# The scans of a stick-breaking attention cut at pairs of key tiles, done in place, and queued across steps

## The chip, the cores and the metric

One core of one Trainium2 chip runs the whole program. Its engines run side by side, each through its own list of instructions in order: TensorE (PE, with its weight loads as PEld), VectorE (DVE), ScalarE (ACT), GpSimd (POOL), and SyncE (SP), which issues most transfers. The metric is the time of one execution in device microseconds (us), the median over several runs.

## The reference

A decoder layer over 1024 tokens of width 1024, in float32: a gated feed-forward half, two attentions side by side, a second feed-forward half, and a gated embedding. The change touches one of the two attentions, the stick-breaking one, with 8 heads of width 64:

```python
def one_block(args):                  # 128 queries against all keys
    qi, pi = args
    z = jnp.einsum('bqhd,bkhd->bhqk', qi, k).astype(jnp.float32) * scale
    mask = kpos[None, :] < pi[:, None]
    log_beta = jax.nn.log_sigmoid(z)
    log_1m = jnp.where(mask, jax.nn.log_sigmoid(-z), 0.0)
    after = lax.cumsum(log_1m, axis=3, reverse=True) - log_1m
    a = jnp.where(mask, jnp.exp(log_beta + after), 0.0)
    return jnp.einsum('bhqk,bkhd->bqhd', a.astype(v.dtype), v)
```

So the weight of key s for query t is sigmoid(z[t,s]) times the product of sigmoid(-z[t,j]) over all keys j between s and t. The kernel has no logarithm: it scans the sigmoid(-z) of a query from its own position back to key 0, as a running product, and multiplies the result with sigmoid(z).

## The kernel before

Products are made of matmuls in a reduced float32 form, with each operand split into a high and a low part, three matmuls for one. The attention part goes over 16 heads (h = 0 to 15), first the 8 of the forgetting attention, then the 8 stick-breaking ones (h = 8 to 15). A head is four steps, c = 0 to 3; step c handles the two query tiles i = 2c and i = 2c + 1, of 128 queries each, against the first (i + 1) * 128 keys. Work is staggered: step c calls `scores` for its own two tiles and then `apply` for the step before it. So `apply` of c = 3 runs in the next head's step c = 0.

`scores`, for each of its two tiles: PE makes z (lines 941 and 942, two matmuls for each stretch of at most 512 keys); ACT writes sigmoid(-z) to G (L949) and sigmoid(z) to T (L950); POOL zeroes what is above the diagonal in T (L956, AFFINE_SELECT); DVE scans G into R (all scans are recorded at L917); POOL multiplies T with R (L964, L968). The scan begins with the 128 keys of the diagonal, which needs a mask tile as second operand, and goes on backwards from there. The scans and multiplications of a tile are cut in two near the middle (`right` and `left`). For the first tile of a step both parts are issued at once; for the second they are put into the list `later` and issued one after each transposition of `apply`.

`apply`, for the step before: for each pair of key tiles, from the last (kpair = c) down to 0, PE transposes four (for kpair = c three) blocks of T into one of two PSUM banks (L993), ACT copies the high part (L995), DVE subtracts for the low part (L996). A bank is free for the next transposition but one when both have read it. Then PE multiplies the transposed weights with the values (L1015); ACT and DVE bring the result into Y (L1037, L1038).

All PE instructions keep the order in which the program states them. The scans, the low parts (L996) and the splits of the finished Y (L105 on ACT, L106 on DVE) are tied in that order on DVE. Other instructions of ACT, DVE and POOL are placed by a planner with its own estimates of time.

Between these pieces PE does other work, the filling: projections for later heads and gate products (L700, L708) and, in the last head, the output projection (L1227). `take` hands it out in portions: a step has 7, 4, 5 and 6 portions for c = 0 to 3, two of them in `scores`, and `share` says which part of the head's filling the step gets. The filling brings work to the other engines: a new weight tile is copied on ACT for its high part (L129) and subtracted on POOL for its low part (L139); a finished product is evacuated (L782 and L783, L828, L830).

In the last two heads finished rows of Y come back from memory and are split into high and low (`split_y`): two in (h = 14, c = 3), two in (15, 0) and three in (15, 1). The buffers they go into are those of the filling's operand; the second pair becomes free when the last L708 matmul has run.

Of the kernel before, what the change touches and what calls it, by code (L numbers as in the profile page):

```python
# [14 lines left out]
ALU = mybir.AluOpType  # L15
# [3 lines left out]
P = 128  # L19
S = 1024  # L20
# [16 lines left out]
def tile_hybrid_decoder_layer(  # L37
# [6 lines left out]
    nc = tc.nc  # L44
# [871 lines left out]
    def scan(*args):  # L916
        order("dve", nc.vector.tensor_tensor_scan(*args))  # L917

    def scores(step, fill, later=None):
        step["pr"] = []  # L920
        Q, KH, KL = step["st"]["st"]
        fox = step["fox"]
        for i in (2 * step["c"], 2 * step["c"] + 1):
            n = (i + 1) * P
            na, w = seg(n)
            d0 = n - P
            T = slot("T", [P, S])
            if fox:
                m = stat([P, 3], "m")
                l = stat([P, 1], "l")  # L930
                fb = step["fb"]["t"]
                nc.gpsimd.tensor_add(T[:, d0:n], fb[:, d0:n], mask_fox[:])
                nm_ = 0
            else:
                G = slot("GF", [P, S])
                R = slot("RN", [P, S])
            for a in range(na):
                c0, c1 = a * w, (a + 1) * w
                ps = bank("sc")
                q = Q[:, i * P:(i + 1) * P]  # L940
                pe(nc.tensor.matmul(ps[:, :w], q, KH[:, c0:c1], start=True, stop=False))  # L941
                pe(nc.tensor.matmul(ps[:, :w], q, KL[:, c0:c1], start=False, stop=True))  # L942
                if fox:
                    for x0, x1, add in ((c0, min(c1, d0), fb), (max(c0, d0), c1, T)):
                        if x0 < x1:
                            nc.vector.tensor_tensor_reduce(T[:, x0:x1], add[:, x0:x1], ps[:, x0 - c0:x1 - c0], -1.0, m[:, nm_ - 1:nm_] if nm_ else 3e38, ALU.add, ALU.min, m[:, nm_:nm_ + 1])
                            nm_ += 1
                else:
                    nc.scalar.activation(G[:, c0:c1], ps[:, :w], AF.Sigmoid, scale=-(HD ** -0.5))  # L949
                    nc.scalar.activation(T[:, c0:c1], ps[:, :w], AF.Sigmoid, scale=HD ** -0.5)  # L950
            if fox:
                nc.scalar.activation(T[:, :n], T[:, :n], AF.Exp, bias=m[:, nm_ - 1:nm_], scale=-1.0, accum_out=l[:])
                nc.vector.reciprocal(l[:], l[:])  # L953
                nc.gpsimd.tensor_mul(T[:, :n], T[:, :n], l[:].broadcast_to([P, n]))  # L954
            else:
                nc.gpsimd.affine_select(T[:, d0:n], T[:, d0:n], [[-1, P]], ALU.is_ge, 0.0, base=-1, channel_multiplier=1)  # L956
                cut = (i + 1) // 2 * P if i > 2 else 0

                def right(T=T, G=G, R=R, n=n, d0=d0, cut=cut):
                    z0 = max(d0, 1)  # L960
                    scan(R[:, z0 - 1:n - 1][:, ::-1], G[:, z0:n][:, ::-1], mask_sb[:, z0 - d0:P][:, ::-1], 1.0, ALU.mult, ALU.max)
                    if d0:
                        scan(R[:, cut:d0 - 1][:, ::-1], G[:, cut + 1:d0][:, ::-1], G[:, cut + 1:d0][:, ::-1], R[:, d0 - 1:d0], ALU.mult, ALU.bypass)
                    nc.gpsimd.tensor_mul(T[:, cut:n - 1], T[:, cut:n - 1], R[:, cut:n - 1])  # L964

                def left(T=T, G=G, R=R, cut=cut):
                    scan(R[:, 0:cut][:, ::-1], G[:, 1:cut + 1][:, ::-1], G[:, 1:cut + 1][:, ::-1], R[:, cut:cut + 1], ALU.mult, ALU.bypass)
                    nc.gpsimd.tensor_mul(T[:, :cut], T[:, :cut], R[:, :cut])  # L968
                parts = [right, left] if cut else [right]
                if i % 2 and later is not None:  # L970
                    later.extend(parts)
                else:
                    for part in parts:
                        part()
            step["pr"].append(T)
            fill()

    def apply(step, fill, later=()):
        c = step["c"]
        v2 = step["v"]["v"]  # L980
        hd = step["head"] % 4
        av = bank("av")
        pts = {}

        def transposes(kpair):
            width = 512 if kpair < c else 384
            ps = bank("pt")
            for kb in (2 * kpair, 2 * kpair + 1):
                for j in range(2):
                    if kb == 2 * c + 1 and j == 0:  # L990
                        continue
                    col = (kb % 2) * 256 + (j * P if kb < 2 * c + 1 else 0)
                    pe(nc.tensor.transpose(ps[:, col:col + P], step["pr"][j][:, kb * P:(kb + 1) * P], identf[:]))  # L993
            pt = slot("PT", [P, 2, 512], F32R)
            high = nc.scalar.copy(pt[:, 0, :width], ps[:, :width])  # L995
            low = nc.vector.tensor_sub(pt[:, 1, :width], ps[:, :width], f(pt[:, 0, :width]))  # L996
            if not step["fox"]:
                order("dve", low)
                order("act", high)
            pts[kpair] = pt  # L1000

        def values(kpair):
            pt = pts[kpair]
            mm = []
            for kb in (2 * kpair, 2 * kpair + 1):
                for b in range(2):
                    c0 = (kb % 2) * 256
                    if kb < 2 * c + 1:
                        mm.append((av[:, 0:256], v2[:, kb, hd, :], pt[:, b, c0:c0 + 256]))
                    else:  # L1010
                        mm.append((av[:, P:256], v2[:, kb, hd, :], pt[:, b, c0:c0 + P]))
            if kpair == c:
                mm = [mm[0], mm[2], mm[3], mm[1]]
            for i, (o, lh, r) in enumerate(mm):
                pe(nc.tensor.matmul(o, lh, r, start=(kpair == c and i == 0), stop=(kpair == 0 and i == 3)))  # L1015

        def turn_and_scan(kpair):
            transposes(kpair)
            if later:
                later.pop(0)()  # L1020
            fill()

        turn_and_scan(c)
        for kpair in range(c - 1, -1, -1):
            turn_and_scan(kpair)
            if kpair + 2 <= c:
                values(kpair + 2)
# [9 lines left out]
        nc.scalar.copy(ys, av[HD:P, :256])  # L1037
        nc.vector.tensor_add(ys, av[0:HD, :256], ys)  # L1038
        if hh == 1 and c == 3 and step["last"] is False:
            nc.sync.dma_start(yd[Y["idx"]], Y["t"][:])  # L1040
# [38 lines left out]
    def attention():  # L1079
# [80 lines left out]
        for h in range(16):  # L1160
            fox = h < 8
            if h % 2 == 0:
                idx = fox_pairs[h // 2] if fox else 4 + (h - 8) // 2
                ys[h // 2] = {"t": slot("Y", [P, S]), "idx": idx}
            head = ys[h // 2]["idx"] % 4 * 2 + h % 2
            v = (vf1, vf0, vs0, vs1)[h // 4]
            load_fb(h + 1)
            total = sum(u[0] for u in fill[h])
            state = [0.0, 0.0, 0]
            share = (7 / 22, 4 / 22, 5 / 22, 6 / 22) if fox else (0.14, 0.19, 0.29, 0.38)  # L1170
            gens = [u[1] for u in fill[h]]

            def take(last=False):
                state[0] += total * share[state[2]] / (7, 4, 5, 6)[state[2]]
                while gens and (last or state[1] < state[0]):
                    cost = next(gens[0], None)
                    if cost is None:
                        gens.pop(0)
                    else:
                        state[1] += cost  # L1180
            for c in range(4):
                y0, y1 = Y_AT.get((h, c), ((), ()))
                split_y(*y0)
                load_y(*y1)
                step = {"fox": fox, "c": c, "head": head, "st": stacks[h], "v": v, "y": ys[h // 2], "last": h == 15}
# [365 lines left out]
```

## Time and profile before

| | us |
|---|---|
| median of 3 runs | 2271.35 (2271.24 to 2271.48) |
| the profiled execution | 2270.28 |
| its span, first to last instruction | 2268.5 |
| PE busy in the span | 2246.3 |
| DVE busy | 1443.7 |
| ACT busy | 961.6 |
| POOL busy | 827.8 |

The profile shows one execution. Its timeline gives each instruction's start and duration in us, with the idle time before it and what ended that idle time in brackets; its groups gather instructions of one line and form, with their count, busy time, mean duration in ns, and idle time before them; its windows give each engine's busy time in a stretch; its chain follows the work that ended last back from the end. A shape 128x256 stands for 128 partitions of 256 elements. The stick-breaking heads lie between 1052 and 1390 us of the span, about 41 us each.

### The profile page before, as it was taken

How to read it: one execution, taken by the hardware profiler on the slowest of the kernel's cores; microseconds unless marked ns; L12 is line 12 of the kernel's file. 1: busy time of each engine (PE TensorE's matmuls, PEld its weight loads, DVE VectorE, ACT ScalarE, POOL GpSimd, SP SyncE). 2: the span in 40 equal slices, each digit the busy share in tenths (PEclk: the TensorE clock that was granted, in tenths of full speed). 3: DMA queues.
4: the chain of work that ended last, by engine and by line, in shares of the span. 5: the costliest groups of instructions: out<-in, count | busy, mean ns of one | idle time of the engine just before them, and what ended most of it. 6: DMA issues, size and time to landing. Idle time of an engine off the chain costs nothing.

```text
span 2268.5 us, 30573 instructions
## 1 busy us (share of the span) xinstructions
PE 2246.3 (99%) x11462; PEld 1910.0 (84%) x11462; DVE 1443.7 (64%) x2167; ACT 961.6 (42%) x1709; POOL 827.8 (36%) x762
## 2 busy tenths in 40 slices
PE   8999999999999999999999999999999999999999
PEld 6888888888899999988888878888888888888888
DVE  8845555688862355556666675889655555778753
ACT  6333333333353445545555564246333333434431
POOL 2444444300033456554556554410544444200121
PEclk9999999999999999999999999999999999999999
DMA  3232323484334332232224245822423232756132
GB/s 140 101 117 87 123 84 125 151 304 169 105 123 130 111 94 76 74 103 74 76 71 130 70 158 174 303 106 64 139 84 126 84 126 83 263 194 215 61 103 84
DMA packets 192774, 283.87 MB, mean 125 GB/s; under 512 B 28137, under 2 KB 110441, under 8 KB 192626
## 3 DMA queue, kind: packets, MB, share of 16 engines
q1 hardware_dynamic: 192624, 281.92, 37.4%
q8 instruction: 90, 1.47, 0.3%
q14 instruction: 58, 0.48, 0.1%
q10 hardware_dynamic: 2, 0.00, 0.0%
HBM read 189.83 MB, written 75.27 MB: 117 GB/s over the span
## 4 chain that ended last, share of the span: by engine, by line
PE 95%; DVE 3%; ACT 1%; issue 1%; DMA 0%; DVEq 0%; ACTq 0%
PE ps L473 35%; PE ps L368 21%; PE ps L708 11%; PE ps L700 8%; PE ps L1494 4%; PE ps L1227 4%; PE ps L1015 3%; PE ps L993 3%; PE ps L942 1%; PE ps L428 1%; PE ps L941 1%; PE ps L860 1%; PE ps L228 1%; DVE H L106 0%; ACT H L105 0%
## 5 line engine op out<-in xcount | busy, mean ns | idle before, releaser
L368 PE MATMUL ps<-H,H 128*128 128x512 f32 x2184 | 497.7, 389 | 1.2 <-DVE X L376 1.2
L368 PEld LDWEIGHTS ps<-H,H 128*128 128x128 f32 x2184 | 409.3, 188 | 86.7 <-issue 2.0
L473 PE MATMUL ps<-H,WL 128*128 128x512 f32 x1008 | 239.3, 389 | 0.8 <-ACT WL L105 0.8
L473 PEld LDWEIGHTS ps<-H,WL 128*128 128x128 f32 x1008 | 189.1, 188 | 40.5 <-ACT WL L105 1.2
L708 PE MATMUL ps<-H,WH 128*128 128x512 f32 x768 | 211.6, 402 | 0.0
L139 POOL TENSOR_TENSOR WL<-RAW,WH 128x512 fp32r<-128x512 f32 (+1 forms) x108 | 127.6, 1205 | 84.9 <-ACT WH L129 71.2
L708 PEld LDWEIGHTS ps<-H,WH 128*128 128x128 f32 x768 | 136.3, 189 | 22.3 <-issue 0.2
L139 POOL TENSOR_TENSOR WL<-Y,WH 128x512 fp32r<-128x512 f32 (+1 forms) x10 | 14.4, 1464 | 382.6 <-ACT WH L129 382.6
L473 PE MATMUL ps<-H,Q 128*128 128x512 f32 x600 | 143.1, 389 | 0.0
L376 DVE SCALAR_TENSOR_TENSOR X<-ps,X 128x512 f32<-128x512 f32 x168 | 109.0, 685 | 50.9 <-PE ps L368 50.9
L996 DVE TENSOR_TENSOR PT<-ps,PT 128x512 fp32r<-128x512 f32 (+1 forms) x160 | 100.7, 631 | 59.7 <-ACT PT L995 59.4
L473 PEld LDWEIGHTS ps<-H,Q 128*128 128x128 f32 x600 | 112.6, 188 | 23.4
L700 PE MATMUL ps<-WH,H 128*128 128x256 f32 (+1 forms) x896 | 129.8, 286 | 0.0
L995 ACT CAST PT<-ps 128x512 fp32r<-128x512 f32 (+1 forms) x160 | 87.1, 546 | 85.3 <-PE ps L993 79.7
L473 PE MATMUL ps<-X,WL 128*128 128x512 f32 x504 | 121.1, 389 | 0.0
L700 PEld LDWEIGHTS ps<-WH,H 128*128 128x128 f32 x896 | 116.7, 190 | 1.0
L473 PEld LDWEIGHTS ps<-X,WL 128*128 128x128 f32 x504 | 94.6, 188 | 19.6
L708 PE MATMUL ps<-H,WL 128*128 128x512 f32 x384 | 106.1, 396 | 0.0
L917 DVE TENSOR_TENSOR_SCAN RN<-GF,RN 128x127 f32<-128x127 f32 (+2 forms) x96 | 103.3, 1076 | 2.7
L954 POOL TENSOR_TENSOR T<-T,l 128x128 f32<-128x128 f32 (+3 forms) x64 | 73.1, 1150 | 87.2 <-DVE l L953 87.0
L1015 PE MATMUL ps<-PT,X 128*128 128x256 f32 (+1 forms) x640 | 98.2, 282 | 3.8 <-DVE PT L996 2.3
L1015 PEld LDWEIGHTS ps<-PT,X 128*128 128x128 f32 x640 | 90.3, 190 | 13.1 <-DVE PT L996 4.1
(396 smaller groups left out, 4629.7 us busy)
## 6 DMA issues: line engine op xcount, KB each, us to landing
hidden<-PT SPq DMA_DIRECT2D x40, 512.0 KB, 3.1
WH<-in_ffn_w_gate_dram SPq DMA_DIRECT2D x38, 512.0 KB, 5.3
Q<-hidden SPq DMA_DIRECT2D x24, 512.0 KB, 6.9
hidden<-RN SPq DMA_DIRECT2D x22, 512.0 KB, 2.6
RAW<-in_w_in_dram SPq DMA_DIRECT2D x22, 512.0 KB, 4.1
KH<-in_ffn_w_up_dram SPq DMA_DIRECT2D x20, 512.0 KB, 6.2
KL<-in_ffn_w_up_dram SPq DMA_DIRECT2D x20, 512.0 KB, 6.7
T<-in_ffn_w_down_dram SPq DMA_DIRECT2D x20, 512.0 KB, 4.2
```

What stands on the lines that cost most here:

```text
L139: ins = eng_lo.tensor_sub(lo[part], raw[part], f(hi[part]))
L368: pe(nc.tensor.matmul(groups[g][t][:], act[:, a, k, t * P:(t + 1) * P], wt[:, b, k, :], start=(fresh and n == 0), stop=(i in (6, 1, 4) and ...
L376: nc.vector.scalar_tensor_tensor(xs, groups[g][t][:], scale, xs, ALU.mult, ALU.add)
L473: pe(nc.tensor.matmul(ps[:], hl[:, a, k, :], rhs(m, b, k), start=(first and i == 0), stop=(final and i == 11), skip_group_check=True))
L700: pe(nc.tensor.matmul(ps[:, :n], hT[t // 4][a][:, k, (t % 4) * P:(t % 4 + 1) * P], w[k // 4][b][:, k % 4, :n], start=(i == 0), stop=(i == ...
L708: pe(nc.tensor.matmul(ps[:], w[a][:, k, :], hT[half][b][:, k, :], start=(i == 0), stop=(i == 23)))
L917: order("dve", nc.vector.tensor_tensor_scan(*args))
L995: high = nc.scalar.copy(pt[:, 0, :width], ps[:, :width])
L996: low = nc.vector.tensor_sub(pt[:, 1, :width], ps[:, :width], f(pt[:, 0, :width]))
L1015: pe(nc.tensor.matmul(o, lh, r, start=(kpair == c and i == 0), stop=(kpair == 0 and i == 3)))
L1227: pe(nc.tensor.matmul(ps[:], w[a][:, k, :], yT[g][b][:, k, half * 512:half * 512 + 512], start=(i == 0), stop=(i == 11)))
L1494: pe(nc.tensor.matmul(ps, hT[t // 4][a][:, k, (t % 4) * P:(t % 4 + 1) * P], pl["w"][d, k // 2][b][:, k % 2, cs], start=(i == 0), stop=(i = ...
```

## The change

R is gone: the scan writes its product over its own operand in G, and G alternates between the two kinds of buffers that G and R had. A tile's scan and its multiplication are cut at every 256 keys (a pair of key tiles) instead of once near the middle. The part of the diagonal (kp = c) is issued at once for both tiles. The other c parts of a tile go into a queue `pend`, which lives across steps and heads and is kept sorted by step and then from the last pair to the first. `pop()` issues the first of the queue: once after each tile in `scores` and once after each transposition in `apply`; `pop(key)` issues all up to a key, so that a pair's parts are ahead of its transposition. The shares of the filling for the stick-breaking heads become 0.22, 0.20, 0.30 and 0.28 for c = 0 to 3. The description of the change also says "with all gates in the filling"; the diff has no line on gates, and the units of the filling and their order are the same.

```diff
+    def pop(upto=None):
+
+        while pend and (upto is None or pend[0][:2] <= upto):
+            pend.pop(0)[2]()
+            if upto is None:
+                break
+
+    pend = []
+
-    def scores(step, fill, later=None):
+    def scores(step, fill):
...
             else:
-                G = slot("GF", [P, S])
-                R = slot("RN", [P, S])
+                G = slot(("GF", "RN")[i % 2], [P, S])
...
-                cut = (i + 1) // 2 * P if i > 2 else 0
-
-                def right(T=T, G=G, R=R, n=n, d0=d0, cut=cut):
-                    z0 = max(d0, 1)
-                    scan(R[:, z0 - 1:n - 1][:, ::-1], G[:, z0:n][:, ::-1], mask_sb[:, z0 - d0:P][:, ::-1], 1.0, ALU.mult, ALU.max)
-                    if d0:
-                        scan(R[:, cut:d0 - 1][:, ::-1], G[:, cut + 1:d0][:, ::-1], G[:, cut + 1:d0][:, ::-1], R[:, d0 - 1:d0], ALU.mult, ALU.bypass)
-                    nc.gpsimd.tensor_mul(T[:, cut:n - 1], T[:, cut:n - 1], R[:, cut:n - 1])
-
-                def left(T=T, G=G, R=R, cut=cut):
-                    scan(R[:, 0:cut][:, ::-1], G[:, 1:cut + 1][:, ::-1], G[:, 1:cut + 1][:, ::-1], R[:, cut:cut + 1], ALU.mult, ALU.bypass)
-                    nc.gpsimd.tensor_mul(T[:, :cut], T[:, :cut], R[:, :cut])
-                parts = [right, left] if cut else [right]
-                if i % 2 and later is not None:
-                    later.extend(parts)
-                else:
-                    for part in parts:
-                        part()
+
+                def part(kp, T=T, G=G, n=n, d0=d0):
+                    c0 = kp * 256
+                    c1 = min(c0 + 256, n)
+                    z0 = max(c0, 1)
+                    if c1 == n:
+                        z1 = max(d0, 1)
+                        g = G[:, z1:n][:, ::-1]
+                        scan(g, g, mask_sb[:, z1 - d0:P][:, ::-1], 1.0, ALU.mult, ALU.max)
+                        if z0 < d0:
+                            g = G[:, z0:d0][:, ::-1]
+                            scan(g, g, g, G[:, d0:d0 + 1], ALU.mult, ALU.bypass)
+                        c1 = n - 1
+                    else:
+                        g = G[:, z0:c1][:, ::-1]
+                        scan(g, g, g, G[:, c1:c1 + 1], ALU.mult, ALU.bypass)
+                    nc.gpsimd.tensor_mul(T[:, c0:c1], T[:, c0:c1], G[:, c0 + 1:c1 + 1])
+                part(step["c"])
+                pend.extend((step["id"], -kp, lambda kp=kp, part=part: part(kp)) for kp in range(step["c"] - 1, -1, -1))
+                pend.sort(key=lambda e: e[:2])
+                pop()
...
         def turn_and_scan(kpair):
             transposes(kpair)
-            if later:
-                later.pop(0)()
+            pop()
+            pop((step["id"], 2 - kpair))
             fill()

+        pop((step["id"], 1 - c))
         turn_and_scan(c)
...
-        for part in later:
-            part()
...
-            share = (7 / 22, 4 / 22, 5 / 22, 6 / 22) if fox else (0.14, 0.19, 0.29, 0.38)
+            share = (7 / 22, 4 / 22, 5 / 22, 6 / 22) if fox else (0.22, 0.2, 0.3, 0.28)
...
-                later = []
                 state[2] = c
-                scores(step, take, later if prev is not None else None)
+                scores(step, take)
                 if prev is not None:
-                    apply(prev, take, later)
+                    apply(prev, take)
                 prev = step
```

More of the change, by code (lines that the diff above doesn't have):

```diff
@@ L975, in scores, with apply @@
+                part(step["c"])
+                pend.extend((step["id"], -kp, lambda kp=kp, part=part: part(kp)) for kp in range(step["c"] - 1, -1, -1))
+                pend.sort(key=lambda e: e[:2])
+                pop()
             step["pr"].append(T)
             fill()
-    def apply(step, fill, later=()):
+    def apply(step, fill):
         c = step["c"]
@@ L1184, in attention @@
                 load_y(*y1)
[L1185 removed]
+                step = {"fox": fox, "c": c, "head": head, "st": stacks[h], "v": v, "y": ys[h // 2], "last": h == 15, "id": 4 * h + c}
                 if fox:
                     step["fb"] = fbs[h]
[L1188 removed]
                 state[2] = c
[L1190 removed]
+                scores(step, take)
                 if prev is not None:
[L1192 removed]
+                    apply(prev, take)
                 prev = step
```

## The prediction

> **What bounds the kernel now.** I read the page's busy times first, then its chain of work, then windows over the stages.
>
> ```profile
> span 2268.5 us, 30573 instructions
> PE 2246.3 (99%) x11462; PEld 1910.0 (84%) x11462; DVE 1443.7 (64%) x2167; ACT 961.6 (42%) x1709; POOL 827.8 (36%) x762
> PE 95%; DVE 3%; ACT 1%; issue 1%; DMA 0%; DVEq 0%; ACTq 0%
> ```
> ```profile
> 755.00:1055.00 300.00, 295.01 (x2099) 274.19 (x2098) 169.60 (x553) 153.27 (x338) 171.16 (x174) 1.00 0.31 85
> 1055.00:1301.00 246.00, 246.00 (x1431) 215.32 (x1430) 165.14 (x228) 132.98 (x277) 141.80 (x157) 1.00 0.33 88
> 1301.00:1392.00 91.00, 87.13 (x466) 73.37 (x465) 64.87 (x88) 56.53 (x113) 46.54 (x53) 1.00 0.52 169
> ```
>
> The window rows give stretch, length, then busy PE, PEld, DVE, ACT, POOL, the clock and DMA. Heads 8 to 13 (1055 to 1301 us) have PE busy without a gap: 246.00 of 246.00, at full clock. The change removes no matmul, so nothing can be won there. Heads 14 and 15 have 91.00 - 87.13 = 3.87 us of idle PE. PE's timeline shows it as two waits, both in head 15, both for a low part; DVE's shows what held that up.
>
> ```profile
> 1335.84 0.22 PE L941 MATMUL ps<-KH,Q 128*128 128x128 f32 x1
> ...
> 1340.89 0.66 PE L993 MATMUL ps<-identf,T 128*128 128x128 f32 x4 [1.56 <-DVE PT L996]
> ...
> 1345.52 0.34 PE L941 MATMUL ps<-KH,Q 128*128 128x384 f32 x1
> ...
> 1351.38 0.45 PE L1015 MATMUL ps<-PT,X 128*128 128x256 f32 x2
> 1354.13 0.50 PE L1015 MATMUL ps<-PT,X 128*128 128x128 f32 x2 [2.31 <-DVE PT L996]
> ```
> ```profile
> 1336.65 0.42 DVE L1038 TENSOR_TENSOR Y<-ps,Y 64x256 f32<-64x256 f32 x1 [2.09 <-ACT Y L1037]
> 1337.60 2.36 DVE L106 TENSOR_TENSOR H<-X,H 128x1024 fp32r<-128x1024 f32 x2 [0.54 <-ACT H L105]
> 1339.88 0.51 DVE L917 TENSOR_TENSOR_SCAN RN<-GF,mask_sb 128x127 f32<-128x127 f32 x1
> 1340.31 0.53 DVE L996 TENSOR_TENSOR PT<-ps,PT 128x384 fp32r<-128x384 f32 x1
> ...
> 1348.37 3.59 DVE L106 TENSOR_TENSOR H<-X,H 128x1024 fp32r<-128x1024 f32 x3 [1.24 <-PE ps L708]
> ...
> 1353.55 0.53 DVE L996 TENSOR_TENSOR PT<-ps,PT 128x384 fp32r<-128x384 f32 x1
> ```
>
> The most that can be gained is 3.87 us, 0.17%; all else is a question of new waits.
>
> **The change part by part.** Prices, from the groups of DVE and POOL in the scans' stretch:
>
> ```profile
> L917 DVE TENSOR_TENSOR_SCAN RN<-GF,mask_sb 128x128 f32<-128x128 f32 x56 | 36.6, 653 | 14.7 <-ACT GF L949 14.6
> ...
> L917 DVE TENSOR_TENSOR_SCAN RN<-GF,RN 128x255 f32<-128x255 f32 x24 | 23.9, 996 | 0.8
> ...
> L996 DVE TENSOR_TENSOR PT<-ps,PT 128x384 fp32r<-128x384 f32 x33 | 18.2, 552 | 14.4 <-ACT PT L995 14.2
> ...
> L917 DVE TENSOR_TENSOR_SCAN RN<-GF,RN 128x256 f32<-128x256 f32 x16 | 12.6, 787 | 0.6
> ...
> L917 DVE TENSOR_TENSOR_SCAN RN<-GF,RN 128x127 f32<-128x127 f32 x16 | 8.0, 502 | 0.6
> ```
> ```profile
> L139 POOL TENSOR_TENSOR WL<-RAW,WH 128x512 fp32r<-128x512 f32 x32 | 43.1, 1367 | 5.6 <-issue 5.3
> ...
> L968 POOL TENSOR_TENSOR T<-T,RN 128x256 f32<-128x256 f32 x16 | 12.1, 754 | 0.0
> L968 POOL TENSOR_TENSOR T<-T,RN 128x512 f32<-128x512 f32 x8 | 10.4, 1295 | 9.3 <-DVE RN L917 9.3
> ```
>
> *More and smaller pieces.* Scans go from 160 to 192 and multiplications from 104 to 160, over the same elements. A scan's fixed part is 502 - 127 * (787 - 502)/129 = 221 ns, so 32 more are 7.1 us of DVE; a multiplication's is 2 * 754 - 1295 = 213 ns, so 56 more are 11.9 us of POOL. Spread over 337 us, with DVE 67% and POOL 58% busy in the second window, both are hidden: 0. Without that cover they would cost the whole 19 us. Scanning in place has no row; I take the rows of G to R (a tenth more or less on 787 ns would be 0.08 us a piece, 24 pieces a head, 1.9 us, beside a DVE idle for a third of the window). Dropping R frees buffers nobody waits for. ACT's and SP's instructions are the same in number; SP only exchanges neighbours.
>
> *The filling.* In the order of PE's instructions, the filling matmuls between the start of a step c = 3 and its third transposition go from 8 + 7 + 8 + 7 = 30 to 5 + 6 + 6 + 5 = 22; in c = 0 from 10 to 16 (head 15: 9 to 14). So c = 3 gets tighter and c = 0 looser.
>
> *The order on DVE.* This decides. In c = 3 the low part after the first transposition came behind the first tile's scans only; now it comes behind the diagonal and second pair of both tiles, so it waits for the second tile's sigmoids:
>
> ```
> before  scan mask 383 384             | low | scan mask 383 | low | 512 | low
> after   scan mask 256, mask 128 256   | low | 256           | low | 256 | low | 255
> ```
>
> Head 10 as measured, its step beginning at 1159.00:
>
> ```profile
> 1159.00 0.37 PE L941 MATMUL ps<-KH,Q 128*128 128x448 f32 x1
> ...
> 1168.38 0.60 PE L993 MATMUL ps<-identf,T 128*128 128x128 f32 x4
> ```
> ```profile
> 1160.95 0.56 ACT L950 ACTIVATE T<-ps 128x448 f32<-128x448 f32 x1
> ...
> 1163.09 0.60 ACT L949 ACTIVATE GF<-ps 128x512 f32<-128x512 f32 x1
> 1163.57 0.62 ACT L950 ACTIVATE T<-ps 128x512 f32<-128x512 f32 x1
> 1164.05 1.07 ACT L129 CAST WH<-RAW 128x1024 fp32r<-128x1024 f32 x1
> ```
> ```profile
> 1161.18 0.65 DVE L917 TENSOR_TENSOR_SCAN RN<-GF,mask_sb 128x128 f32<-128x128 f32 x1 [0.90 <-ACT GF L949]
> ...
> 1165.53 0.56 DVE L996 TENSOR_TENSOR PT<-ps,PT 128x384 fp32r<-128x384 f32 x1 [1.59 <-ACT PT L995]
> ```
> ```profile
> 1069.05 1.62 PE ps L708 x7
> ```
>
> The third transposition stood at 9.38 us into the step and needed the low part, done at 7.09. A filling matmul takes 1.62/7 = 0.231 us, so it now stands at 9.38 - 8 * 0.231 = 7.53. The second tile's G is ready at 4.69. From there: mask 0.42 (row below), 128 as the 127 row 0.50, 256 0.75, low 0.55: done at 6.9. That fits by 0.6 us, in heads 9, 11 and 13. In heads 8, 10 and 12 ACT's new order puts the weight copy (1.07) between the two tiles' sigmoids. The first tile's end at 2.51, the copy near 3.5, then three sigmoids follow, starting 0.48 us apart and lasting 0.62: G is ready near 5.1. POOL's two weight pieces come behind the first tile's multiplications (its mask scan ended at 2.83, the 256 scan follows to 3.6, the multiplication of 754 ns to 4.4), just when DVE scans. What such a meeting costs stands in head 12:
>
> ```profile
> 1234.89 2.64 POOL L139 TENSOR_TENSOR WL<-RAW,WH 128x512 fp32r<-128x512 f32 x2
> ```
> ```profile
> 1235.05 1.41 DVE L917 TENSOR_TENSOR_SCAN RN<-GF,mask_sb 128x128 f32<-128x128 f32 x1
> 1236.49 1.59 DVE L917 TENSOR_TENSOR_SCAN RN<-GF,RN 128x255 f32<-128x255 f32 x1
> ```
> ```profile
> 1176.83 0.42 DVE L917 TENSOR_TENSOR_SCAN RN<-GF,mask_sb 128x128 f32<-128x128 f32 x1
> ...
> 1183.25 0.75 DVE L917 TENSOR_TENSOR_SCAN RN<-GF,RN 128x255 f32<-128x255 f32 x1
> ```
>
> Beside the weights' pieces the two scans took 1.41 and 1.59, alone 0.42 and 0.75: each waited for the piece ahead of it. So in heads 8, 10 and 12 the low part ends between 5.1 + 0.42 + 0.50 + 0.75 + 0.55 = 7.3 (no meeting, no wait) and 5.1 + 1.41 + 1.59 + 0.75 + 0.55 = 9.4 (a wait of 1.9). As the pieces would start near 4.4 and last 2.64, I take the middle, a little up: 1.1 us each, 3.3 in all. Behind the late low part DVE has the next low parts and scans, which PE needs some 2 us later, at the values. Head 14 has smaller weights, but an evacuation (L783) ahead of the low part: 0 to 1.7, taken 0.6.
>
> Here the Trainium skill says the same more strictly. Its page "SBUF — State Buffer", section "Who interferes with whom", states that a VectorE instruction with two SBUF inputs and a GpSimd instruction that reads SBUF exclude each other, the later waiting for the whole of the earlier. The trace agrees with exclusion in the 1.41 and 1.59 us above, but the second weight piece started while the mask scan was still shown as running (2.64 us for two): the ends overlap. By the strict rule the sum would be that of the third rival, not mine.
>
> *c = 0.* Before its first low part DVE now has one 255 scan left from c = 3 and the second tile's two scans more: 0.75 + 0.42 + 0.50 = 1.67 us later, up to 2.15 at mean prices (996 ns for the 255 form elsewhere). PE arrives 6 * 0.231 = 1.39 us later. Undisturbed heads showed no wait: 0.0 to 0.4 each, taken 0.2 in all. Head 15 begins with two splits and had no slack: 1.56 + 1.67 - 5 * 0.231 = 2.1, up to 3.4 with POOL's selections and multiplications between the scans; taken 2.7.
>
> *c = 1 of head 15.* The three splits waited for the last L708 matmul, 2.85 us into the step. With 24 filling matmuls in c = 0 that matmul is over 0.4 us before the step. From first split to the end of the low part took 1354.08 - 1348.37 = 5.71; one mask, one 128 and the Y addition (0.42) come in, 1.3, with POOL's turns up to 2.5: done at 6.6 to 7.8. PE gets there at 1351.82 - 1345.52 + 2 * 0.231 = 6.76. Wait 0 to 1.1, taken 0.6, for 2.31.
>
> **Sum.** New waits 3.3 + 0.6 + 0.2 + 2.7 + 0.6 = 7.4, gone 3.87: +3.5 us. The profiled execution would go from 2270.28 to 2273.8. It is 1.07 us under the median of 2271.35, so the median comes to 2274.9.
>
> **The rivals.** *No new wait in c = 3*: the weights arrive elsewhere or the scans slip between. For: heads 9, 11 and 13 fit by 0.6. Then 0.2 + 2.7 + 0.6 - 3.87 = -0.4, so 2271.0. *Faster*: head 15's two waits go as well, because the looser c = 0 covers all scans and the splits run early; it decides if the first low part of (15, 0) ends within PE's time to the third transposition (1340.89 - 1.56 - 1335.84 + 5 * 0.231 = 4.6). Against it: the splits alone ended 4.1 us into that step. 2271.35 - 3.87 = 2267.5. *Slower, strict exclusion*: with scans and multiplications cut smaller, each piece on DVE waits for a whole one on POOL. It decides from 8.4 us of waits in all. Against it: the overlapping ends. Then c = 3 with weights 1.9 * 3 and head 14 1.7, six heads' c = 0 at 0.4, head 15 3.4 + 1.1 and again 1.7 in its c = 3: 16.0 - 3.87 = +12.1, 2283.5. *Filling starved*: weights late for L708, against which speaks that no PE wait for them shows in these heads.
>
> **How the numbers follow.** My case 0.50 (own range 2272.5 to 2277.5), no new wait 0.22, strict exclusion 0.18, faster 0.06, starved 0.04. The bound of 0.2%, about what a measurement here tells from no change, is 4.5 us: 2266.8 to 2275.9. My case splits 0.33 within and 0.17 slower; no new wait lies within (0.20, and 0.02 faster by things not seen), faster gives 0.04 within and 0.02 beyond; the other two are slower. Faster 0.04, same 0.57, slower 0.39. The range for 8 in 10, from the quiet case's lower end to part of the strict one: 2269.6 to 2281.
>
> **What would show it.** PE waits at the third transposition (L1004) for the low part (L1007) in c = 3 of heads 8, 10, 12 and 14, of 0.5 to 1.9 us; one near 2.7 in (15, 0); less than 1.1 in (15, 1); none in heads 9, 11 and 13. I am wrong if heads 8 to 13 still show PE busy throughout, or if PE waits for POOL's T.

## The result and the profile after

The changed kernel took 2275.34 us (median of 21 runs, 2273.77 to 2276.1) against 2271.28 for the kernel before (21 runs beside it): 1.0017 times as long, 95% interval 1.0011 to 1.0024. So it is 4 us slower; forecast were 3.5 us and 2274.9 us. The runs of both kernels fall in two groups about 1.5 us apart, of which the last section tells more; the execution in the profile, of 2274.2 us, is of the lower group.

The busy times and the chain of the page after:

```profile
span 2272.4 us, 30706 instructions
...
PE 2248.0 (99%) x11462; PEld 1911.1 (84%) x11462; DVE 1433.2 (63%) x2199; ACT 960.9 (42%) x1709; POOL 824.6 (36%) x818
...
PE 94%; DVE 4%; ACT 2%; issue 1%; DMA 0%; POOL 0%; ACTq 0%; DVEq 0%
```

DVE does 32 instructions more in 10 us less, POOL 56 more in 3 us less, and the kernel is slower: the sums of the engines decide nothing here. The windows over heads 8 to 13 and over heads 14 and 15 (the latter 4 us longer than the stretch shown of before, since these heads end later), with busy PE, PEld, DVE, ACT, POOL, the clock and DMA:

```profile
1055.00:1301.00 246.00, 242.97 (x1407) 211.52 (x1405) 151.77 (x247) 130.56 (x274) 138.59 (x194) 1.00 0.32 86
1301.00:1396.00 95.00, 90.19 (x490) 76.30 (x488) 67.33 (x103) 58.53 (x116) 50.03 (x73) 1.00 0.52 165
```

PE, without a gap in heads 8 to 13 before, now idles 3.03 us there, and 4.81 in heads 14 and 15 for 3.87. It stands in six rows of PE's timeline (L1004 is the transposition, L1007 the low part and L1026 the values: L993, L996 and L1015 of the kernel before):

```profile
1087.45 0.63 PE L1004 MATMUL ps<-identf,T 128*128 128x128 f32 x4 [0.81 <-DVE PT L1007]
...
1171.06 0.63 PE L1004 MATMUL ps<-identf,T 128*128 128x128 f32 x4 [1.41 <-DVE PT L1007]
...
1253.42 0.63 PE L1004 MATMUL ps<-identf,T 128*128 128x128 f32 x4 [0.81 <-DVE PT L1007]
...
1335.39 0.63 PE L1004 MATMUL ps<-identf,T 128*128 128x128 f32 x4 [0.42 <-DVE PT L1007]
...
1346.76 0.63 PE L1004 MATMUL ps<-identf,T 128*128 128x128 f32 x4 [2.32 <-DVE PT L1007]
...
1360.47 0.49 PE L1026 MATMUL ps<-PT,X 128*128 128x128 f32 x2 [2.06 <-DVE PT L1007]
```

The first four are the third transposition in c = 3 of heads 8, 10, 12 and 14, the others lie in (15, 0) and (15, 1). Together 7.83 us, less the 3.87 of before: +3.96, and the span grew by 3.9. Heads 9, 11 and 13 have none. That the two figures agree to 0.1 is partly luck. A wait of the kernel before, in (8, 0) and just ahead of the windows, is gone too:

```profile
1054.65 0.66 PE L993 MATMUL ps<-identf,T 128*128 128x128 f32 x4 [0.39 <-DVE PT L996]
```

And PE's first wait of all, for the input, is 4.0 us where the profiled execution of before had 4.5. So part of the growth lies in no marked wait: PE is busy for 1.7 us longer with as many matmuls.

Why the even heads wait and the odd ones don't is seen in ACT, POOL and DVE of head 10 (its step begins at 1161.95) and PE and DVE of head 11 (1204.13):

```profile
1164.34 1.07 ACT L129 CAST WH<-RAW 128x1024 fp32r<-128x1024 f32 x1
```
```profile
1166.16 2.65 POOL L139 TENSOR_TENSOR WL<-RAW,WH 128x512 fp32r<-128x512 f32 x2
```
```profile
1166.99 0.73 DVE L917 TENSOR_TENSOR_SCAN RN<-RN,mask_sb 128x128 f32<-128x128 f32 x1 [1.60 <-ACT RN L957]
1167.76 2.11 DVE L917 TENSOR_TENSOR_SCAN RN<-RN 128x128 f32<-128x128 f32 x2
1169.79 0.67 DVE L783 TENSOR_TENSOR KL<-ps,KH 128x512 fp32r<-128x512 f32 x1
1170.37 0.55 DVE L1007 TENSOR_TENSOR PT<-ps,PT 128x384 fp32r<-128x384 f32 x1
...
1208.50 0.42 DVE L917 TENSOR_TENSOR_SCAN RN<-RN,mask_sb 128x128 f32<-128x128 f32 x1 [0.93 <-ACT RN L957]
1208.96 1.35 DVE L917 TENSOR_TENSOR_SCAN RN<-RN 128x128 f32<-128x128 f32 x2
1210.23 0.53 DVE L1007 TENSOR_TENSOR PT<-ps,PT 128x384 fp32r<-128x384 f32 x1
```
```profile
1211.69 0.60 PE L1004 MATMUL ps<-identf,T 128*128 128x128 f32 x4
```

In head 10 the second tile's scans begin 5.04 us into the step, in head 11 4.37: the weight copy L129 stands between the two tiles' sigmoids. And beside the weights' pieces on POOL the scans take 0.73 and 2.11 us, for 0.42 and 1.35.

### The profile page after: what moved, and what is told of

Read it like the earlier page. It is cut to its first block, busy times and chain, and to the rows that moved or that the text cites. A ratio compares the mean times of both kernels' runs of the same rounds, so it can differ in the third digit from the quotient of the medians.

```text
span 2272.4 us, 30706 instructions
## 1 busy us (share of the span) xinstructions
PE 2248.0 (99%) x11462; PEld 1911.1 (84%) x11462; DVE 1433.2 (63%) x2199; ACT 960.9 (42%) x1709; POOL 824.6 (36%) x818
## 4 chain that ended last, share of the span: by engine, by line
PE 94%; DVE 4%; ACT 2%; issue 1%; DMA 0%; POOL 0%; ACTq 0%; DVEq 0%
PE ps L473 35%; PE ps L368 21%; PE ps L708 11%; PE ps L700 8%; PE ps L1503 4%; PE ps L1236 4%; PE ps L1026 3%; PE ps L1004 3%; PE ps L950 1%; PE ps L949 1%; PE ps L428 1%; PE ps L860 1%; PE ps L228 1%; DVE H L106 1%; DVE RN L917 1%
## 5 line engine op out<-in xcount | busy, mean ns | idle before, releaser
L1007 DVE TENSOR_TENSOR PT<-ps,PT 128x512 fp32r<-128x512 f32 (+1 forms) x160 | 100.4, 630 | 56.8 <-ACT PT L1006 56.2
L1006 ACT CAST PT<-ps 128x512 fp32r<-128x512 f32 (+1 forms) x160 | 87.3, 547 | 93.2 <-PE ps L1004 86.0
L1026 PE MATMUL ps<-PT,X 128*128 128x256 f32 (+1 forms) x640 | 98.0, 282 | 3.5 <-DVE PT L1007 2.1
L1026 PEld LDWEIGHTS ps<-PT,X 128*128 128x128 f32 x640 | 90.4, 190 | 12.3 <-DVE PT L1007 3.6
L269 POOL TENSOR_TENSOR PT<-GF,RN 128x512 f32<-128x512 f32 x20 | 33.1, 1656 | 186.0 <-DVE GF L516 186.0
```

## The experiments

Each time stands against a median of 2271.2 to 2271.3 us of the kernel before on the same chip. Where an edit adds lines, what follows stands a few lines further down: L1006, L1008 or L1009 is then the transposition, L1011 or L1012 the low part, L1030 or L1031 the values, L922 the scan, L144 the weights' low part and L107 the split.

**The old shares.** The change is two things, new scans and new shares of the filling. First the new scans alone:

```diff
-            share = (7 / 22, 4 / 22, 5 / 22, 6 / 22) if fox else (0.22, 0.2, 0.3, 0.28)
+            share = (7 / 22, 4 / 22, 5 / 22, 6 / 22) if fox else (0.14, 0.19, 0.29, 0.38)
```

> The changed kernel with the old division of the filling (0.14, 0.19, 0.29, 0.38): the pairs of key tiles, in place and queued, but without the new shares. My theory: the wait of the third transposition in c = 3 needs both the later low part and the shorter filling ahead of it, so with 30 filling matmuls there again it goes: none in heads 8, 10, 12 and 14 (3.3 us less than in the changed kernel). Head 15 gets worse, because c = 0 and c = 1 are again short of filling: 3.2 us in (15, 0) (the 1.56 of before plus 1.67 of more scans) and 3.5 to 4.5 in (15, 1). Time about 2274.5, between the changed kernel's 2275.3 and 2272. Rival, the division alone costs (POOL and DVE shut each other out whatever the filling): the waits in c = 3 stay near 0.8 us each and the time goes to 2277 or more.

Measured: 2283.88 us, 1.0058 times before (1.0044 to 1.0071). The waits in c = 3 are gone, as expected, but others came in c = 0 of heads 9 and 11 to 14 and one of 0.97 us in (10, 2), of which the two longest (heads 12 and 14) stand here with those of (15, 0) and (15, 1):

```profile
1221.44 0.63 PE L1004 MATMUL ps<-identf,T 128*128 128x128 f32 x4 [1.34 <-DVE PT L1007]
...
1304.78 0.63 PE L1004 MATMUL ps<-identf,T 128*128 128x128 f32 x4 [1.34 <-DVE PT L1007]
...
1348.74 0.63 PE L1004 MATMUL ps<-identf,T 128*128 128x128 f32 x4 [3.43 <-DVE PT L1007]
...
1365.89 0.80 PE L1026 MATMUL ps<-PT,X 128*128 128x128 f32 x2 [4.88 <-DVE PT L1007]
```

The eight waits after 1055 us add up to 12.67, 8.80 more than before, and the span is 13.7 us longer. Most of the remainder is in the clock: from 1.3 to 4.7 us after the wait of 3.43 us PE was busy throughout, but at half speed, as windows behind it show (the clock stands third from the end):

```profile
1348.50:1350.00 1.50, 1.26 (x10) 1.22 (x10) 0.69 (x2) 0.59 (x1) 0.42 (x1) 1.00 0.09 36
...
1350.50:1353.50 3.00, 3.00 (x14) 2.81 (x13) 0.90 (x2) 0.59 (x1) 0.00 (x0) 0.50 0.00 0
```

Some 3.3 us at half clock cost 1.6, and PE's half clock around the end of the wait of 4.88 costs some 2.3 more. What follows: my theory holds for c = 3, and nearly for (15, 0), but it missed c = 0 of the other heads and the clock, and with them the time by 9 us; the rival's time is reached, though not by its waits in c = 3. The divided scans need the longer c = 0.

**The new shares alone.** The same line, in the kernel before:

```diff
-            share = (7 / 22, 4 / 22, 5 / 22, 6 / 22) if fox else (0.14, 0.19, 0.29, 0.38)
+            share = (7 / 22, 4 / 22, 5 / 22, 6 / 22) if fox else (0.22, 0.2, 0.3, 0.28)
```

> The kernel before with the new division of the filling alone (0.22, 0.2, 0.3, 0.28); scans as before. My theory: the shares are a gain and the order of the scans is the loss. In c = 3 the low part ends 7.1 us into the step and PE arrives at 7.5, so no wait there; the wait in (15, 0) falls from 1.56 to about 0.4, since 5 more filling matmuls of 0.231 us stand ahead of it, and the one in (15, 1) from 2.31 to 0.2 to 1.0, since the last L708 matmul then comes before that step. Time about 2268.5. Rival, the shorter filling in c = 3 is what costs: waits of 0.4 to 1.4 us in c = 3 here as well, and 2272 to 2275.

Measured: 2271.53 us, 1.0003 (0.9995 to 1.0012): nothing. Head 15 did get better ((15, 0) 1.05, (15, 1) none), but the shorter filling in c = 3 uncovers the low parts further on, which the values wait for, in heads 10 and 12 twice each (0.74 and 0.63) and in (15, 3). These are the rival's waits in c = 3, at another place, and the time is 0.5 us below its range:

```profile
1171.83 0.62 PE L1015 MATMUL ps<-PT,X 128*128 128x256 f32 x3 [0.74 <-DVE PT L996]
...
1379.55 0.62 PE L1015 MATMUL ps<-PT,X 128*128 128x256 f32 x3 [1.22 <-DVE PT L996]
```

So the gain that my theory had did not come. Alone, by the medians, the shares cost nothing and the division 12.6 us (some 4 us of that run are the half clock); together they cost 4.1. So the shares give back 8.5 us of what the division takes. Against the lower group of the kernel before, near 2269.8, the shares alone cost 1.7 us.

**The diagonal queued too.** To move the second tile's scans away from the front of the low part:

```diff
-                part(step["c"])
-                pend.extend((step["id"], -kp, lambda kp=kp, part=part: part(kp)) for kp in range(step["c"] - 1, -1, -1))
+                if i % 2 == 0:
+                    part(step["c"])
+                pend.extend((step["id"], -kp, lambda kp=kp, part=part: part(kp)) for kp in range(step["c"] - (i + 1) % 2, -1, -1))
                 pend.sort(key=lambda e: e[:2])
-                pop()
+                if i % 2 == 0:
+                    pop()
```

> The changed kernel, but the second tile's diagonal part is no longer issued at once: it goes into the queue like the others, and one queued part is taken after the first tile only. So ahead of the first low part in c = 3 DVE has the first tile's scans alone. My theory (the low part waits because the second tile's sigmoids and scans stand ahead of it on DVE): the waits in c = 3 of heads 8, 10, 12 and 14 go (3.3 us), those in head 15 become about 1.2 in (15, 0) and 1.0 to 2.0 in (15, 1): 2270 to 2271.5. Rival (the pieces of the weights on POOL are the cause, wherever the scans stand): some wait of 0.5 to 1 us stays in each of heads 8, 10 and 12, and the time stays above 2273.5.

Measured: 2292.3 us, 1.0093 (1.0079 to 1.0107). Neither theory: PE now waits for POOL's products. Its waits of that stretch in one row (us, times, longest), and one of them beside the multiplication that ended it:

```profile
PE ps L1006 <- POOL T L981: 16.5, 36, 2.4
```
```profile
1087.34 0.33 PE L1006 MATMUL ps<-identf,T 128*128 128x128 f32 x1 [0.92 <-POOL T L981]
```
```profile
1086.30 0.99 POOL L981 TENSOR_TENSOR T<-T,GF 128x256 f32<-128x256 f32 x1
```

By the program, steps c = 1, 2 and 3 issue one, two and two parts less than they queue, so up to five are left for the step that transposes them; in the changed kernel it is one at most. The low part does come earlier, as no wait for it is left after 1055 us; but a part that is issued no step ahead puts POOL's multiplication in PE's way.

**The weights without their low part.**

```diff
+        if bare[0]:
+            hi = whigh(wraw_load(pieces, nk, n), nk, n, tags[0])
+            return hi, hi
...
```

`bare` is set in the stick-breaking heads, here and in the next run.

> The changed kernel with the low parts of the filling's weights left out in the stick-breaking heads: the high part is used in their place, so the product of the weights' low part is not computed, the matmuls are the same in number, and POOL has no pieces of weights beside the scans. ACT's weight copy then also mostly moves behind the sigmoids. My theory (what the weights do in c = 3 is the difference between the even heads and the odd ones, and what they do in (15, 1) is why that wait was 2.06 and not 0.6): the waits in heads 8, 10 and 12 go, (15, 1) falls to 0.6 or less, (15, 0) stays near 2: time about 2270.5 to 2271.5. Rival (the later place of the low part alone makes the wait, and the weights add little): waits of 0.4 us and more stay in c = 3 of the even heads, and the time is 2273.5 or more.

Measured: 2270.36 us, 0.9995 (0.9986 to 1.0003). The waits in c = 3 are all gone, head 14's too; (15, 0) is unmoved, and (15, 1) goes a third of the way expected. The time is 0.1 us below the range expected. PE's two rows, and the first split and the low part of (15, 1) on DVE:

```profile
1342.17 0.63 PE L1008 MATMUL ps<-identf,T 128*128 128x128 f32 x4 [2.32 <-DVE PT L1011]
...
1356.95 0.50 PE L1030 MATMUL ps<-PT,X 128*128 128x128 f32 x2 [1.56 <-DVE PT L1011]
```
```profile
1348.98 2.36 DVE L107 TENSOR_TENSOR H<-X,H 128x1024 fp32r<-128x1024 f32 x2 [2.66 <-PE ps L712]
...
1356.37 0.52 DVE L1011 TENSOR_TENSOR PT<-ps,PT 128x384 fp32r<-128x384 f32 x1
```

From first split to the end of the low part it is 7.91 us here, 8.78 in the changed kernel: the weights' pieces are 0.87 of it, not all that was missing.

**A quarter of the low part.** The last run took the pieces away and moved ACT's copy behind the sigmoids too. This one leaves the copy where it is:

```diff
+        if bare[0]:
+            nk //= 4
+            raw, hi = raw[:, :nk], hi[:, :nk]
         lo = slot(tag, [P, nk, n], F32R)
...
```

> The changed kernel with the low part of the filling's weights made for a quarter of the rows only in the stick-breaking heads, and that quarter used for all rows: the rest of the weights' low part is left out of the product. ACT's order is that of the changed kernel, with the weight copy between the two tiles' sigmoids, and POOL's pieces are a quarter as long (0.66 us for two, for 2.64). It parts the copy from the pieces. My theory (the pieces lengthen the scans by some 1 us, the copy starts them 0.67 us later, and only the two together miss PE): waits in c = 3 of heads 8 and 12 gone, 0.2 to 0.4 left in head 10 with its evacuation (L783) ahead of the low part, 0 to 0.4 in head 14; (15, 0) stays near 2.3, (15, 1) 1.5 as without pieces: about 2272.2. Rival (the place of the copy is the cause): 0.5 to 0.9 us stay in heads 8 and 12 and over 1 in head 10: 2274.5 or more.

Measured: 2270.12 us, 0.9998 (0.9989 to 1.0007). Heads 8, 12 and 14 have no wait, head 10 has 0.35; (15, 0) 2.33 and (15, 1) 1.48. Head 10 again, PE, POOL and DVE:

```profile
1168.48 0.63 PE L1009 MATMUL ps<-identf,T 128*128 128x128 f32 x4 [0.35 <-DVE PT L1012]
```
```profile
1164.63 0.87 POOL L144 TENSOR_TENSOR WL<-RAW,WH 128x128 fp32r<-128x128 f32 x2
```
```profile
1165.47 0.42 DVE L922 TENSOR_TENSOR_SCAN RN<-RN,mask_sb 128x128 f32<-128x128 f32 x1 [1.60 <-ACT RN L962]
1165.93 1.36 DVE L922 TENSOR_TENSOR_SCAN RN<-RN 128x128 f32<-128x128 f32 x2
```

From the mask scan to the end of the low part it takes 2.87 us, 3.93 in the changed kernel. So the meeting with the pieces costs 1.06 (beside the quarter ones the scans take what they take in head 11), and the wait fell by 1.41 - 0.35 = 1.06. The late copy alone is within PE's slack, except where the evacuation L783 comes in as well. The waits are those expected; the time is 2 us less than expected, as six of the eleven runs lie in the lower of two groups.

**The splits spread.** Head 15's splits of Y, one, one, two and one for c = 0 to 3 in place of two and three:

```diff
-    Y_AT = {(14, 0): ((), range(4)), (14, 3): ((0, 1), (4, 5)), (15, 0): ((2, 3), (6,)), (15, 1): ((4, 5, 6), ())}
+    Y_AT = {(14, 0): ((), range(4)), (14, 3): ((0, 1), (4, 5)), (15, 0): ((2,), (6,)), (15, 1): ((3,), ()), (15, 2): ((4, 5), ()), (15, 3): ((6,), ())}
```

> The changed kernel with the splits of Y spread over head 15: one in c = 0, one in c = 1, two in c = 2 and one in c = 3, where the changed kernel has two in c = 0 and three in c = 1. My theory (head 15's two waits are the splits' time on DVE, 1.2 us a split, ahead of the low part): (15, 0) from 2.32 to about 1.1, (15, 1) from 2.06 to 0, new waits of 0 to 0.8 in (15, 2) and none in (15, 3); c = 3 of the other heads unchanged: 2272.0 to 2272.8. Rival (the scans of both tiles alone make those waits): (15, 0) above 1.7 and (15, 1) above 1, and less than 1 us gained.

Measured: 2270.98 us, 1.0000 (0.9991 to 1.0009). (15, 0) fell to the row below and (15, 1) to nothing, no wait came in their place, and c = 3 stayed as it was, to the hundredth.

```profile
1345.51 0.63 PE L1004 MATMUL ps<-identf,T 128*128 128x128 f32 x4 [1.21 <-DVE PT L1007]
```

The waits are 3.17 us less and the median is 4.4 less, 1 us below the range expected: the section on the hardware has the rest.

**The second tile behind the low part.** The repair of the queued diagonal, with as many parts in each step as in the changed kernel:

```diff
-                part(step["c"])
-                pend.extend(...)
+                def turn(kp=step["c"], part=part, step=step):
+                    part(kp)
+                    pend.extend(...)
...
+                if i % 2 and later is not None:
+                    later.append(turn)
+                else:
+                    turn()
...
             transposes(kpair)
+            if later:
+                later.pop(0)()
             pop()
...
```

> The changed kernel, but the second tile's turn (its diagonal part and one part taken from the queue) comes on DVE right behind the low part of the first transposition, not ahead of it. Unlike the kernel with the queued diagonal, as many parts as before are issued in each step, so none comes in the step that needs it. My theory (the wait is the second tile's scans ahead of the first low part): waits in c = 3 of heads 8, 10, 12 and 14 gone (3.45 us), (15, 0) from 2.32 to about 1.1, (15, 1) from 2.06 to about 0.9: 2269.5 to 2270.5. Rival (DVE's sum between two transpositions is what counts, so the wait goes to the next low part or to the values): 0.5 to 1 us in each of those steps again, 2272.5 or more. A third way, PE waits for POOL's T as with the queued diagonal: 2278 or more.

Measured: 2270.11 us, 0.9996 (0.9987 to 1.0005). No third transposition waits in c = 3, and (15, 1) has no wait; shorter ones, of 0.24 to 0.50, came at the values in heads 9, 10, 11, 13 and 15, and (15, 0) has more than expected. The longest of the former and (15, 0):

```profile
1202.62 0.62 PE L1031 MATMUL ps<-PT,X 128*128 128x256 f32 x3 [0.50 <-DVE PT L1012]
...
1344.25 0.63 PE L1009 MATMUL ps<-identf,T 128*128 128x128 f32 x4 [1.60 <-DVE PT L1012]
```

The time is the one expected, and the order on DVE is the cause, but the rival has a part too: of 7.83 us 3.49 stay, 1.89 of them moved to the values.

**Both edits together.** The last two in one kernel:

> The two last edits together: the second tile's turn behind the first low part, and the splits of Y spread over head 15. My theory: the gains add, as they lie in different steps: c = 3 free of waits, head 15 with 0 to 0.8 in all: 2267.5 to 2268.5, under the kernel before. Rival (the waits only move along DVE): 2271 or more.

Measured: 2269.04 us, 0.9991 (0.9983 to 1.0000), with 2.25 us of waits, none above 0.50. That is 0.5 us above the range expected: the gains add only in part. Apart, the two edits took away 4.34 and 3.17 us of waits, together 5.58. Each removes the wait of 2.06 in (15, 1), which can go but once: 4.34 + 3.17 - 2.06 = 5.45.

**The spread in the kernel before.** The same line of Y in the kernel before:

> The kernel before with the splits of Y alone spread over head 15 (one in c = 0, one in c = 1, two in c = 2, one in c = 3); scans and shares of the filling as before. My theory: its two waits in head 15, 1.56 and 2.31, are the splits' and go to 0.4 and 0, with 0 to 0.8 new in (15, 2) and nothing in heads 8 to 13. And the runs of the kernel before lie in two groups, near 2269.8 and 2271.4, the upper one at a mean clock of 0.999, as do all kernels here with a PE wait of 2.3 us or more and none with less: so this kernel's runs lie in one group, all together 2266.2 to 2267.5. Rival (the splits' DVE time only moves its wait to c = 2 and c = 3): 2268.5 or more.

Measured: 2267.75 us, 0.9986 (0.9977 to 0.9995), all 11 runs between 2267.65 and 2267.91. This is the version that beats both kernels. The wait in (15, 0) is 0.43 and the one in (15, 1) gone. New are two, of 1.13 and 0.41, of a kind that no theory had: PE waits to reuse the filling's bank, which the gate's multiplication (L1234) reads late, as it stands behind two splits on DVE. The time is 0.25 us above the range expected. The longer wait, and what stood ahead of it on DVE:

```profile
1355.38 0.50 PE L1227 MATMUL ps<-H,WH 128*128 128x512 f32 x1 [1.13 <-DVE Q L1234]
```
```profile
1350.45 3.38 DVE L106 TENSOR_TENSOR H<-X,H 128x1024 fp32r<-128x1024 f32 x2
...
1354.66 0.66 DVE L1234 TENSOR_TENSOR Q<-Q,ps 128x512 f32<-128x512 f32 x1
```

**Old shares with the later turn and the spread.** The kernel with both edits, and the old shares:

> The changed kernel with the second tile's turn behind the first low part, the splits of Y spread, and the old division of the filling (0.14, 0.19, 0.29, 0.38). My theory (the division of the scans needs the new shares only because the second tile's scans stand ahead of the first low part; behind it, c = 0 does with 10 filling matmuls): the waits that the old shares gave in c = 0 of heads 9 to 14 (0.2 to 1.3 each) don't come, those of 0.25 to 0.5 at the values in c = 3 go, (15, 0) has up to 1.5: 2267 to 2268.5. Rival (the divided scans need the longer c = 0 wherever they stand): waits of 0.5 us and more in c = 0 or c = 1 of several heads: 2270 or more.

Measured: 2270.93 us, 1.0000 (0.9991 to 1.0009), a miss. The waits of c = 0 in heads 12 and 14 shrank to pairs of 0.16 and 0.20 us, so their cause was found, but with 1.09 in (15, 0), 0.78 at the filling's bank and smaller ones the waits still sum to 3.51. By that the span would be 0.4 under before; it is 0.4 above, 2268.9. Most of these 0.8 us can lie in waits too short to be marked: in c = 3 of heads 8 and 12 the eight value matmuls took 1.46 us, for 1.09 to 1.12 in the other steps and in the kernel before.

```profile
1088.02 1.46 PE L1031 MATMUL ps<-PT,X 128*128 128x256 f32 x8
```

**New shares with the spread,** in the kernel before:

> The kernel before with the new shares and the splits of Y spread; scans as before. My theory: the 2.74 us of waits at the values in c = 3 of heads 10 and 12 stay, (15, 0) goes from 1.05 to 0, and (15, 3), which had 1.22 without a split of its own, gets up to 1.2 more: 2270 to 2271.5, above the kernel before with the spread alone. Rival (with the spread the new shares pay): under 2268.5.

Measured: 2271.69 us, 1.0004 (0.9995 to 1.0012). As my theory had it, heads 10 and 12 keep 2.78 us of waits and (15, 0) none; (15, 3) keeps 1.24 without getting more, and 0.80 came in (15, 2) instead. The time is 0.2 us above the range expected: the new shares are no gain to the old scans, even without head 15's crowding.

## Why the prediction was right

*That the sums on DVE and POOL cost nothing* held: both engines' busy time even fell. A 128x256 product on POOL, priced at a mean of 754 ns, took 663 (by GF) and 680 (by RN) in mean, and a scan of 256 in place 906 in GF and 775 in RN, on the two sides of the 787 taken.

*Nothing to win in heads 8 to 13* held but for the 0.39 us in (8, 0), which the prediction's window left out, and the order on DVE decided. *c = 3 of heads 8, 10 and 12*, taken at 1.1 each, measured 0.81, 1.41 and 0.81: 3.03 for 3.3. The quarter weights show both halves of the reason: the late copy takes up the slack, and the pieces add 1.06, close to the middle chosen between no meeting and two full ones. Missed was that head 10 has an evacuation (0.67) ahead of its low part, the one instruction that heads 8 and 12 don't have there. That 3.03 came so close is partly luck: the missed 0.60 of head 10 made up for two heads that waited 0.29 less than taken. *Head 14* measured 0.42 for 0.6. Heads 9, 11 and 13 have no wait, as said, and by the way that was forecast: in head 11 the third transposition stands 7.56 us into the step (forecast 7.53) and the low part ends at 6.63 (6.9).

*c = 0*, taken at 0.2, had no new wait, but only by the new shares: with the old ones 0.2 to 1.3 us appeared there. *(15, 0)* measured 2.32 for 2.7; taking one split out lowered it by 1.11, about a split's 1.18.

*(15, 1)*, taken at 0.6 with a ceiling of 1.1, measured 2.06, and this is the step that failed. PE got there 6.54 us into the step, close to the 6.76 forecast. DVE, from the first split:

```profile
1351.64 2.90 DVE L106 TENSOR_TENSOR H<-X,H 128x1024 fp32r<-128x1024 f32 x2 [1.32 <-PE ps L708]
1354.47 0.41 DVE L1048 TENSOR_TENSOR Y<-ps,Y 64x256 f32<-64x256 f32 x1
1354.81 1.42 DVE L106 TENSOR_TENSOR H<-X,H 128x1024 fp32r<-128x1024 f32 x1
1356.15 0.51 DVE L917 TENSOR_TENSOR_SCAN GF<-GF,mask_sb 128x128 f32<-128x128 f32 x1
1356.69 0.75 DVE L917 TENSOR_TENSOR_SCAN GF<-GF 128x255 f32<-128x255 f32 x1
...
1359.15 0.82 DVE L917 TENSOR_TENSOR_SCAN RN<-RN 128x255 f32<-128x255 f32 x1
1359.89 0.53 DVE L1007 TENSOR_TENSOR PT<-ps,PT 128x384 fp32r<-128x384 f32 x1
```

There are two 255 scans ahead of the low part, one before the change: the forecast added a mask scan, a 128 scan and the Y addition, and left out this one (0.75). The other 0.87 is the weights' pieces, which in this kernel come beside the splits (2.90 us for two, 2.36 without pieces) and before came behind them. 7.01 + 0.75 + 0.87 = 8.63 of the 8.78 measured.

The sum came out at 7.83 for 7.4, since the terms that were too high (c = 3, head 14, c = 0, (15, 0): 1.03 together) made up for most of the 1.46 that (15, 1) was too low. That part is luck, and so is some of the median: the forecast carried over the 1.07 us between the profiled execution of before and its median, but this distance is mostly a matter of which group of runs each lies in. Of the changed kernel's 21 runs 11 lie in the upper group; with one fewer the median would have been near 2274.4. Of the rivals, *no new wait in c = 3* is ruled out by the first row of waits, *faster* by those of head 15, and *filling starved* by all six, since no PE wait there is for weights. *Strict exclusion*, 2283.5 us, did not come: the waits stayed under its 1.9 in every c = 3. The Trainium skill's rule behind it ("SBUF — State Buffer", section "Who interferes with whom") has scans and pieces of this kind shut each other out. The trace agrees in that scans beside the pieces are longer (0.73 and 2.11 us for 0.42 and 1.35); the waits that the rival built on it were not reached.

## What to carry to other kernels

When an engine's list is kept in order, price a change by what stands ahead of the one instruction that the bounding engine waits for, piece by piece, and not by the engine's sum: with 10 us less on DVE this kernel is 4 us slower. A new order and the filling that covers it belong together: by the medians they cost 12.6 and 0 us alone and 4.1 together, so costs found one by one don't add. And look for what crowds one step before rearranging all of them: spreading the five splits of head 15 over its four steps, one line, gained 3.5 us, which no version of the new scans did.

## What the runs showed of the hardware

A wait of PE can cost more than its length. In the run without the weights' low part, behind the wait of 2.32 us in (15, 0), PE was at half clock for 3.5 us, which costs 1.7:

```profile
1343.50:1347.00 3.50, 3.50 (x15) 3.11 (x15) 1.34 (x2) 1.99 (x3) 0.00 (x0) 0.52 0.02 5
```

In the changed kernel's profile the same wait was followed by full clock (the wait ends at 1346.76):

```profile
1346.50:1350.50 4.00, 3.74 (x26) 3.47 (x27) 2.10 (x4) 2.59 (x5) 0.44 (x1) 1.00 0.03 9
```

The runs agree with a fall that comes in some executions only: 33 of the kernel before fall in two groups, 9 near 2269.8 us at a mean clock of 1.000 and 24 near 2271.4 at 0.999 or 0.998, those of the changed kernel too (10 near 2274.15, 11 near 2275.6), and also the two without full low weights. All these have a wait between 2.3 and 2.4 us. With the queued diagonal, whose longest wait is 2.42 us, the profile has 3.4 us at half clock as well, and its four runs lie in one group at 0.999. The kernels whose longest wait is 1.6 us or less (new shares alone, spread splits, later turn) each lie in one group; single runs of them are listed at 0.999 too (three of eleven with spread splits), so the groups of times say more here than this rounded mean. The kernel before with the spread fell into one group below the lower of its two, as expected. So the spread's 3.5 us are about 2 of waits and 1.5 of clock. That a wait of this length is the cause was not tested by a wait made for it alone.

The Trainium skill's page "TensorE: Matmul & The Clock Gate", section "Part 1: The HAM clock gate (the "warmup" mystery)", has the half clock, a window of about 3.4 us and says that this window runs freely, so that the place of a change differs from run to run. These rows agree with that (0.50 to 0.52 for 3.0 to 3.5 us); the page puts the fall after an idle window of about 3.4 us, while here 2.3 us were enough in some executions.

The other size not expected: two pieces of weights of 128x256 on POOL, 1.43 us with DVE idle just ahead of (15, 0), took 3.46 beside the splits of (15, 1), and the first two splits took 2.90 there, for 2.36 without pieces.

```profile
1339.62 1.43 POOL L139 TENSOR_TENSOR WL<-RAW,WH 128x256 fp32r<-128x256 f32 x2 [0.23 <-issue]
...
1351.69 3.46 POOL L139 TENSOR_TENSOR WL<-RAW,WH 128x256 fp32r<-128x256 f32 x2 [4.74 <-ACT H L105]
```
